# Projection of the per-layer inputs: from the last stage into the prompt's gated linear attention

## The chip, the cores and the metric

The kernel runs on one core of a Trainium2 chip. Its time is the device time of one execution in microseconds (us). A core has a matrix engine (TensorE, here PE, with its weight loads shown apart as PEld), a vector engine (DVE), a scalar engine (ACT), a general engine (POOL), and a sync engine (SP), which here issues most transfers. Each works through its own instructions in order and waits on semaphores for the others.

## What is computed

The program is one step of a decoder layer over a prompt of 1024 tokens and a sample of 8 x 8 tokens: an input projection, gated linear attention (GLA, 4 heads) beside latent attention (8 heads, for the sample over a paged cache of 8192 positions), an output projection, a gated MLP with a short convolution, and at the end the per-layer inputs:

```python
def layer_forward(h, p, pos, gla_s0, conv_prev, attend, lw):
    ...
    o_gla, s_new = gla_chunked(q, k, v, log_a, gla_s0)
    ...
    h = h + jnp.concatenate([o_gla, o_mla], axis=-1) @ lw['w_o']
    y, conv_new = conv_ffn(rmsnorm(h, lw['g_ffn']), conv_prev, lw)
    h = h + y
    h = h + (p.astype(h.dtype) @ lw['ple_w_proj']) * jax.nn.sigmoid(rmsnorm(h, lw['g_ple']) @ lw['ple_w_gate'])
    return h, ckv, krope, s_new, conv_new
```

The product `p @ ple_w_proj` (1024 x 256 by 256 x 1024 for the prompt, 64 x 256 by 256 x 1024 for the sample) depends on nothing else in the layer; its gate depends on nearly everything.

## The kernel before

All matrices are float32. Most products are made of three matmuls of a shorter float32 kind: each operand is split into a high and a low part (`split`, lines 115 to 117: ACT writes the high part, DVE or POOL subtracts), and `mm3` (lines 138 to 141) adds high x high, high x low and low x high in one PSUM bank. Lines 139 to 141 therefore stand for products all over the kernel; one tells them apart by the tile that they write: `ks` (the sample's scores over the cache), `ps_gu` and `ps_dn` (the MLP), `ps_pg` (the last gate), `ps_pj` (the projection, in the last stage).

Two streams are interleaved when the program is written. `dense` is the prompt's work up to the end of its latent attention: the projections in two halves, then GLA, then 8 heads of attention. `cache_stream` is the sample's attention over 64 blocks of the cache; a block has 48 `ks` matmuls with transposes (`ctp`), rope scores (`crp`, `csr`), a softmax (`mt`, `phl`) and a product with the values (`cpv`). Every `yield` of `dense` hands out a weight, and the cache stream takes a step whenever its due time, a step's price times `PACE` of the part, is behind the sum of the weights. The instructions are then ordered on each engine by the scheduler, which moves work of one stream past the other where buffers allow.

GLA runs inside `dense`. `gla_prompt` works on 8 tiles of 128 tokens: `pre` (gates and decays of tile t + 2; loads of gaT, qk and gv), `local` (scores within tile t + 1), `advance` (output `po` and state `pk` of tile t, load of gg), `gla_put` (transposes `pt_go`, store to doT). `gla_sample` is mixed into it a step at a time from the third yield on (`n > GS0`, line 1379). Both take PSUM banks by `pd`, which has three (pool psD); the prompt's attention uses the same three by `pat`.

When `dense` ends, the output projection (`wo_units`, tile `ps_dn`) fills in beside the remaining cache blocks, then come the MLP's two halves (`ff_chunk`, and the seven products of the down projection, tile `ps_dn` again), and then the last stage. Its work on the per-layer inputs stands in three places: `ple_in` loads p (tile `pin`), transposes it (`pt_pl`) and splits it into ph and pl, twice, within the last of the seven products; `ple_proj` loads and splits 256 columns of `ple_w_proj` (wjh, wjl); `ple_unit` does two tiles of 128 tokens and 256 columns at a time: 24 matmuls a tile into `ps_pg`, the sigmoid, 6 matmuls a tile into `ps_pj`, then a multiply and an add on DVE and the store of y_p. `ple_sample` does the same for the sample with 16 + 4 matmuls into one bank. The loop at the end goes over 4 groups of columns, each with 4 pairs of tiles and the sample. All loads and stores there are on SP's queue.

Of the kernel before, what the change touches and what calls it, by code (L numbers as in the profile page):

```python
# [18 lines left out]
P = 128  # L19
D = 1024  # L20
# [25 lines left out]
def step_kernel(ctx: ExitStack, tc: tile.TileContext, A):  # L46
# [46 lines left out]
    doT = dram.tile([D, T], F32, name="doT")  # L93

# [1029 lines left out]

    def gla_prompt(g, wa2, gout, mq, mk):
# [237 lines left out]
    def dense():  # L1363
# [9 lines left out]
        with ExitStack() as s2:  # L1373
            g, g2 = (s2.enter_context(tc.tile_pool(name=nm, bufs=2, reuse_waits="tile")) for nm in ("g", "g2"))
            z["part"] = 4
            sample = gla_sample(g, wa2, *z["gla"])
            for n, w in enumerate(gla_prompt(g2, wa2, *z["gla"])):
                yield w
                if n > GS0:
                    z["part"] = 5  # L1380
                    w2 = next(sample, None)
                    if w2 is not None:
                        yield w2
            for w in sample:
                yield w
# [620 lines left out]
    def ple_in(c):  # L2006

        th, tl = (z["fq"].tile([P, T], F32R, tag="p" + s, name="p" + s, bufs=2) for s in "hl")
        cs = slice(c * P, (c + 1) * P)
        for t0 in (0, 4, 8):  # L2010
            pin = stage([P, 4, P], F32, "pin")
            if t0 < NT:
                n, rows = 4, P
                sp.dma_start(pin, A["p_prompt"][0, 0, t0 * P:(t0 + 4) * P, cs].rearrange("(i p) c -> p i c", p=P))
            else:
                n, rows = 1, R
                sp.dma_start(pin[:R, 0], A["p_sample"][0].rearrange("b t c -> (b t) c")[:, cs])
            pt = p2t([P, 512], "pt_pl")
            w = (n - 1) * P + rows
            for i in range(n):  # L2020
                pe.transpose(pt[:, i * P:i * P + rows], pin[:rows, i], ident[:rows, :rows])
            if t0 < NT:
                split(th[:, t0 * P:t0 * P + w], tl[:, t0 * P:t0 * P + w], pt[:, :w])
            else:
                ts = z["fq"].tile([P, P], F32R, tag="pts", name="pts", bufs=2)
                split(ts[:, :R], ts[:, R:], pt[:, :R])
        return th, tl, ts

# [13 lines left out]
    xn, pT, wpl = {}, [], None  # L2042
    for i, (p, k) in enumerate(steps):
# [28 lines left out]
        elif p == 2:  # L2072
# [6 lines left out]
            if k in (5, 7):  # L2079
                pT.append(ple_in(k // 7))  # L2080
# [21 lines left out]
    def ple_proj(c):  # L2102
        return wload(z["pl"], A["ple_w_proj"][0][:, c * 256:(c + 1) * 256], 2, 256, "wj", 2, st=stg)

    def ple_unit(c, ts, ws):
# [3 lines left out]
        (wj, wg), n = ws, len(ts)  # L2109
# [103 lines left out]
```

## Time and profile before

The profile is of one execution. Its span is what the engines show; the measured time includes a little around it.

| | us |
|---|---|
| runs of the kernel | 2241.42, 2242.73, 2244.2 (median 2242.73) |
| the profiled execution, measured | 2243.74 |
| its span | 2242.0 |
| first output of GLA's prompt tiles (`po`) to the last | 460.6 to 633.6 |
| first and last head's first transpose in the prompt's attention | 651.1, 990.8 |
| first `ps_dn` of the output projection | 1065.1 |
| first `ps_pg`, last `ps_pj` | 2106.7, 2237.8 |

A row of engine time says how long instructions of an engine overlapped the stretch. Matmuls are pipelined, so a row's duration (0.28 us for 256 columns) is longer than the step from one start to the next; what a matmul costs is that step. The PEld share is the time in which weights were being loaded, one load for each matmul.

### The profile page before, as it was taken

The page shows a single profiled execution, that of the slowest core. Times are in us where ns is not written, and L with a number is a line of the kernel's source. Part 1 is how long each engine was busy: PE and PEld are TensorE (multiplying, and loading weights), DVE is VectorE, ACT ScalarE, POOL GpSimd, SP SyncE. Part 2 cuts the span into 40 slices and gives each one's busy share as a digit, 9 for nine tenths or more (in the row PEclk, how much of TensorE's full clock was granted, in tenths as well). Part 3 has the DMA queues.
Part 4 walks back from the last instruction along what each step waited for, and adds up shares of the span by engine and source line. Part 5 has one row for each costly group of instructions (what it writes and reads, how often), then busy time and mean ns, then how long its engine had stood idle before and what let it go on. Part 6 is the DMA issues. An engine that isn't in the chain of part 4 may idle for free.

```text
span 2242.0 us, 38332 instructions
## 1 busy us (share of the span) xinstructions
PE 2140.5 (95%) x13459; PEld 1932.5 (86%) x13459; DVE 1674.3 (75%) x2542; ACT 1360.7 (61%) x3692; POOL 1232.3 (55%) x1320
## 2 busy tenths in 40 slices
PE   7999989999999999999999988999999999998999
PEld 6889978878888888887888877999999998876899
DVE  4775766467788888886878888888888877976632
ACT  5576766777778898887777765434333334434521
POOL 5675667576777777776545558665656560002000
PEclk9899999999999999999999998999999999999999
DMA  5343235413242222212422132323232327667321
GB/s 179 108 144 104 82 115 160 130 56 86 85 126 66 60 60 69 63 56 72 138 78 74 55 117 63 108 90 100 89 100 85 104 72 243 228 173 217 99 77 37
DMA packets 204354, 233.59 MB, mean 104 GB/s; under 512 B 42238, under 2 KB 146147, under 8 KB 204163
## 3 DMA queue, kind: packets, MB, share of 16 engines
q1 hardware_dynamic: 188387, 180.01, 25.6%
q0 software_dynamic: 14544, 46.67, 7.2%
q10 hardware_dynamic: 1232, 4.46, 0.5%
q8 instruction: 108, 1.77, 0.3%
q14 instruction: 83, 0.68, 0.1%
HBM read 188.52 MB, written 42.52 MB: 103 GB/s over the span
## 4 chain that ended last, share of the span: by engine, by line
PE 76%; DVE 8%; ACT 5%; DMA 5%; POOL 3%; issue 2%; SPq 0%; ACTq 0%; DVEq 0%; POOLq 0%
PE ps_gu L140 7%; PE ps_gu L141 7%; PE ps_gu L139 7%; PE ks L139 5%; PE ks L141 4%; PE ks L140 4%; PE cpv L645 2%; PE ctp L522 2%; PE ps_dn L140 2%; PE ps_dn L141 2%; PE ps_dn L139 2%; PE ps_pj L139 2%; PE ps_lt L278 2%; PE ps_pj L140 1%; PE ps_pj L141 1%
## 5 line engine op out<-in xcount | busy, mean ns | idle before, releaser
L560 ACT ACTIVATE csq<-ks 128x256 f32<-128x256 f32 x1040 | 392.5, 400 | 86.7 <-PE ks L141 77.6
L565 DVE TENSOR_REDUCE css<-csq 128x16 f32<-128x1024 f32 (+1 forms) x264 | 315.6, 1196 | 64.6 <-ACT csq L560 63.5
L116 ACT CAST wh<-st 128x512 fp32r<-128x512 f32 x176 | 108.3, 619 | 184.9 <-PE ps_gu L140 164.3
L139 PE MATMUL ks<-mv0h,cTh 128*128 128x320 f32 (+1 forms) x520 | 171.5, 332 | 6.5 <-ACT csq L560 2.9
L139 PE MATMUL ks<-mv1h,cTh 128*128 128x320 f32 (+1 forms) x520 | 169.0, 327 | 7.7 <-ACT sn L562 3.6
L604 POOL TENSOR_TENSOR chl<-craw,chl 128x1024 fp32r<-128x1024 f32 x64 | 141.3, 2207 | 57.2 <-ACT chl L603 56.6
L140 PE MATMUL ks<-mv0l,cTh 128*128 128x320 f32 (+1 forms) x520 | 152.7, 295 | 0.0
L140 PE MATMUL ks<-mv1l,cTh 128*128 128x320 f32 (+1 forms) x520 | 152.6, 295 | 0.0
L141 PE MATMUL ks<-mv0h,cTl 128*128 128x320 f32 (+1 forms) x520 | 148.3, 298 | 0.9 <-DVE cTl L117 0.8
L141 PE MATMUL ks<-mv1h,cTl 128*128 128x320 f32 (+1 forms) x520 | 148.2, 299 | 0.1
L630 POOL TENSOR_TENSOR phl<-sn,phl 128x512 fp32r<-128x512 f32 (+1 forms) x64 | 84.9, 1327 | 106.5 <-ACT phl L629 106.0
L117 DVE TENSOR_TENSOR wl<-st,wh 128x512 fp32r<-128x512 f32 x132 | 119.0, 903 | 28.4 <-ACT wh L116 28.4
L140 PE MATMUL ps_dn<-o 128*128 128x512 f32 x308 | 122.9, 399 | 8.8 <-DVE o L117 8.6
L117 POOL TENSOR_TENSOR wl<-st,wh 128x512 fp32r<-128x512 f32 x44 | 69.5, 1581 | 105.0 <-ACT wh L116 105.0
L141 PE MATMUL ps_dn<-o 128*128 128x512 f32 x308 | 121.2, 394 | 0.0
L117 DVE TENSOR_TENSOR cTl<-ctp,cTh 128x512 fp32r<-128x512 f32 (+1 forms) x136 | 90.0, 662 | 38.9 <-ACT cTh L116 38.0
L562 ACT COPY sn<-ks 128x64 f32<-128x64 f32 x520 | 116.6, 224 | 0.0
L139 PEld LDWEIGHTS ks<-mv0h,cTh 128*128 128x128 f32 x520 | 98.6, 190 | 20.6 <-ACT sn L562 7.3
L139 PEld LDWEIGHTS ks<-mv1h,cTh 128*128 128x128 f32 x520 | 98.5, 189 | 19.7 <-ACT sn L562 7.5
L139 PE MATMUL ps_dn<-o 128*128 128x512 f32 x308 | 109.9, 395 | 5.5 <-ACT o L116 5.5
L1317 POOL TENSOR_TENSOR pl<-p,ph 128x512 fp32r<-128x512 f32 (+1 forms) x96 | 97.4, 1019 | 31.3 <-DVE ph L1316 21.3
L141 PE MATMUL ps_gu<-xrh,wl 128*128 128x320 f32 x352 | 108.7, 309 | 0.0
(674 smaller groups left out, 7881.1 us busy)
## 6 DMA issues: line engine op xcount, KB each, us to landing
raw<-ds SPq DMA_DIRECT2D x77, 256.0 KB
raw<-ffn_w_down SPq DMA_DIRECT2D x66, 256.0 KB
stage<-w_in SPq DMA_DIRECT2D x48, 256.0 KB
st<-ffn_w_gate SPq DMA_DIRECT2D x44, 256.0 KB
st<-ffn_w_up SPq DMA_DIRECT2D x44, 256.0 KB
wr<-ffn_w_down SPq DMA_DIRECT2D x44, 256.0 KB
ds<-cv SPq DMA_DIRECT2D x21, 512.0 KB
oraw<-doT SPq DMA_DIRECT2D x16, 256.0 KB
```

Source lines behind the costliest of these rows:

```text
L116: act.copy(hi, src)
L117: (lo_eng or dve).tensor_tensor(lo, src, hi.bitcast(F32), ALU.subtract)
L139: pe.matmul(ps, ah, bh, start=first, stop=False)
L140: pe.matmul(ps, ah, bl, start=False, stop=False)
L141: return pe.matmul(ps, al, bh, start=False, stop=last)
L278: pe.matmul(ps, x, w, start=first, stop=last)
L560: act.activation(sq[:, f * 256:f * 256 + 256], ks[:, 0:256], AF.Square)
L562: act.copy(o.sn[:, g0 + i, :], ks[:, 256:320])
L565: dve.tensor_reduce(o.ss[:, g0 + i + 1 - n:g0 + i + 1, :].rearrange("p i h -> p (i h)"), sq2[:, :n].rearrange("p i (h n) -> p (i h) n", n= ...
L604: pool.tensor_tensor(ch[:, c0:c1, 128:256], src, ch[:, c0:c1, 0:128].bitcast(F32), ALU.subtract)
L630: pool.tensor_tensor(phl[:, :nt, 64:128], sb, phl[:, :nt, 0:64].bitcast(F32), ALU.subtract)
L1317: pool.tensor_tensor(pl[:, c0:], p[:, c0:], ph[:, c0:].bitcast(F32), ALU.subtract)
```

## The change

The projection of the prompt and the sample is made during GLA by a new generator, `ple_project`, in products of 512 columns; the result goes to two DRAM scratch tensors, `dpj` and `dpjs`. Its weights (2 halves of 512 columns, high and low) take the place of two tiles of `gla_sample` that are done (`qms`, `Ss`), its other tiles rotate with those of `gla_sample` (`gsig`, `gsq`, `go`), and its PSUM banks come from `pd`. In `dense`, once `gla_sample` has nothing left, every yield of `gla_prompt` is followed by two steps of the generator, and what is left runs after it. All its yields have weight 0, so that the cache stream's due times against GLA are as before. In the last stage `ple_in`, `ple_proj` and the `ps_pj` products are gone; `ple_load` reads the product back (tile `pj`, four buffers), two units ahead, and the multiply reads it from there. The loop is written over one list of units, with the same order.

```diff
+    dpj, dpjs = dram.tile([T, D], F32, name="dpj"), dram.tile([R, D], F32, name="dpjs")
...
+    def ple_project(g):
+
+        w = [g.tile([P, 2, 2, 512], F32R, tag=tag, name="wj", bufs=1) for tag in ("qms", "Ss")]
+        for f in range(2):
+            for k in range(2):
+                raw = g.tile([P, 512], F32, tag="gsig", name="wjr")
+                sp.dma_start(raw, A["ple_w_proj"][0][k * P:(k + 1) * P, f * 512:f * 512 + 512])
+                split(w[f][:, 0, k], w[f][:, 1, k], raw, (dve, pool)[k])
+        yield 0.0
+        for t0 in range(0, NT + 1, 2):
+            n, rows = (2, P) if t0 < NT else (1, R)
+            pin = g.tile([P, 2, 256], F32, tag="gsig", name="pin")
+            if t0 < NT:
+                sp.dma_start(pin, A["p_prompt"][0, 0, t0 * P:(t0 + 2) * P, :].rearrange("(i p) c -> p i c", p=P))
+            else:
+                sp.dma_start(pin[:R, 0], A["p_sample"][0].rearrange("b t c -> (b t) c"))
+            for i in range(n):
+                pt = pd([P, 2, P], "pt_pl")
+                for k in range(2):
+                    pe.transpose(pt[:, k, :rows], pin[:rows, i, k * P:(k + 1) * P], ident[:rows, :rows])
+                x = g.tile([P, 2, 2, P], F32R, tag="gsq", name="pT")
...
+                for f in range(2):
+                    ps = pd([P, 512], "ps_pl")
+                    for k in range(2):
+                        if t0 < NT:
+                            mm3(ps, x[:, 0, k], x[:, 1, k], w[f][:, 0, k], w[f][:, 1, k], k == 0, k == 1)
+                        else:
+                            for s_ in range(2):
+                                pe.matmul(ps, x[:, 0, k], w[f][:, s_, k], start=k + s_ == 0, stop=k + s_ == 2)
+                    o = g.tile([P, 512], F32, tag="go", name="pjo")
...
+                        if f:
+                            dve.tensor_copy(o, ps)
+                        else:
+                            act.copy(o, ps)
+                        sp.dma_start(dpj[(t0 + i) * P:(t0 + i + 1) * P, cs], o)
+                    yield 0.0
...
             sample = gla_sample(g, wa2, *z["gla"])
+            early = ple_project(g)
             for n, w in enumerate(gla_prompt(g2, wa2, *z["gla"])):
                 yield w
                 if n > GS0:
...
                     if w2 is not None:
                         yield w2
+                    else:
+                        for _ in range(2):
+                            yield next(early, 0.0)
             for w in sample:
                 yield w
+            for w in early:
+                yield w
...
-            if k in (5, 7):
-                pT.append(ple_in(k // 7))
...
+    def ple_load(c, ts):
+
+        cs, pj = slice(c * 256, c * 256 + 256), pj_room()
+        if ts:
+            t0, n = ts[0], len(ts)
+            sp.dma_start(pj[:, :n], dpj[t0 * P:(t0 + n) * P, cs].rearrange("(i p) c -> p i c", p=P))
+        else:
+            sp.dma_start(pj[:R, 0], dpjs[:, cs])
+        return pj
...
-        for i, t in enumerate(ts):
-            for k in range(2):
-                mm3(pj[:, i], *(x[:, t * P:(t + 1) * P] for x in pT[k][:2]), wj[0][:, k], wj[1][:, k], k == 0, k == 1)
...
+    pjs = [ple_load(c, ts) for c, n, ts in units[:2]]
+    wg = wpl
+    for i, (c, n, ts) in enumerate(units):
+        if i + 2 < len(units):
+            pjs.append(ple_load(units[i + 2][0], units[i + 2][2]))
...
+            ple_unit(c, ts, wg, pjs[i])
```

On PE the first place is GLA, around the state update `pk` of a tile after the sample's work is done. Before:

```order
L1198 MATMUL po<-S,qtb_6135 128x128
L1040 MATMUL pk<-gv,ke 64x128 x4
L1030 MATMUL pt_go<-ident,go 128x128
L139 MATMUL ks<-mv0h,cTh 128x256
L140 MATMUL ks<-mv0l,cTh 128x256
L141 MATMUL ks<-mv0h,cTl 128x256
```

and in the changed kernel, with the projection's `ps_pl` (its lines are numbered one to some fifty higher):

```order
L140 MATMUL ks<-mv0h,cTh 128x320
L141 MATMUL ks<-mv0l,cTh 128x320
L142 MATMUL ks<-mv0h,cTl 128x320
L142 MATMUL ps_pl<-wj,pT 128x512
L140 MATMUL ps_pl<-wj,pT 128x512
L141 MATMUL ps_pl<-wj,pT 128x512
L142 MATMUL ps_pl<-wj,pT 128x512
L1041 MATMUL pk<-gv,ke 64x128 x4
L523 MATMUL ctp<-ident,craw 128x128 x4
```

Four of the projection's matmuls now stand between the tile's output and its state update, together with more `ks` matmuls than before.

The second place, on PE too, is the last head of the prompt's attention, from the second half of its first operand's transposes (`t<-ident,ldq`) on. Before:

```order
L1262 MATMUL t<-ident,ldq 96x128 x4
L522 MATMUL ctp<-ident,craw 128x128 x3
L139 MATMUL ks<-mv1h,cTh 128x256
L140 MATMUL ks<-mv1l,cTh 128x256
L141 MATMUL ks<-mv1h,cTl 128x256
L139 MATMUL ks<-mv1h,cTh 128x320
L140 MATMUL ks<-mv1l,cTh 128x320
L141 MATMUL ks<-mv1h,cTl 128x320
```

and now:

```order
L1310 MATMUL t<-ident,ldq 96x128 x4
L1370 MATMUL o<-ph,vo_9702 128x512
L1371 MATMUL o<-ph,vo_9702 64x512
L1370 MATMUL o<-ph,vo_9702 128x512
L1371 MATMUL o<-ph,vo_9702 64x512
L1310 MATMUL t<-ident,ldk 96x128 x4
L140 MATMUL csr<-qbd0h,kTh 128x64
L141 MATMUL csr<-qbd0l,kTh 128x64
L142 MATMUL csr<-qbd0h,kTl 128x64
```

The `ks` matmuls that went along with the last head before have been placed earlier, in GLA; the last head now stands with hardly any.

More of the change, by code (lines that the diff above doesn't have):

```diff
@@ L2004, in ple_gate @@
                       "gu", 2, st=stg) for i in range(2)]
[L2006 to L2027, printed above, removed]
     z["xs"].tile([P, 2, 512], F32, tag="r", name="raw2", bufs=5)
@@ new lines, in step_kernel @@
+    pjs = [ple_load(c, ts) for c, n, ts in units[:2]]
[3 more added lines that the diff above has]
+            pjs.append(ple_load(units[i + 2][0], units[i + 2][2]))
+        if n == 0 and c:
+            wg = nxt
+        if ts:
+            ple_unit(c, ts, wg, pjs[i])
+        else:
+            ple_sample(c, wg, pjs[i])
+        if c == 0 and n < 2:
+            for t in (2 * n, 2 * n + 1):
+                turned(t, xn[t])
+                if not n:
+                    xn[t + 2] = normalised(t + 2)
+        if c == 1 and n == 1:
+            conv_out()
+        if n == 1 and c < 3:
+            nxt = ple_gate(c + 1)
```

61 lines of the change are left out of this document (26 added, 35 removed).

## The prediction

> **What bounds the kernel now.** The page comes first, for the span and for how much of it each engine is busy.
>
> ```profile
> span 2242.0 us, 38332 instructions
> PE 2140.5 (95%) x13459; PEld 1932.5 (86%) x13459; DVE 1674.3 (75%) x2542; ACT 1360.7 (61%) x3692; POOL 1232.3 (55%) x1320
> ```
>
> TensorE (PE) is busy for 95% of the span, but the ends of its matmuls are modelled; the weight loads (PEld) at 86% leave room. How much, and where, is read from the busy time by stretches: the last six tiles of the prompt's gated linear attention (545 to 651 us), five heads of the latent attention beside the cache stream (736 to 991), the end of that attention (1024.4 to 1052.6), and the last stage (2106 to 2238).
>
> ```profile
> core 0: us, PE busy (x) PEld busy (x) DVE busy (x) ACT busy (x) POOL busy (x), PEclk, DMA share, GB/s
> 545.00:651.00 106.00, 104.35 (x779) 90.62 (x779) 83.65 (x142) 81.18 (x266) 73.47 (x95) 1.00 0.36 97
> 736.00:991.00 255.00, 250.06 (x1721) 218.37 (x1720) 212.88 (x351) 222.76 (x665) 188.15 (x192) 1.00 0.23 65
> 1024.40:1052.60 28.20, 24.23 (x128) 19.34 (x126) 16.06 (x27) 16.76 (x35) 23.08 (x23) 0.88 0.14 38
> 2106.00:2238.00 132.00, 132.00 (x1101) 131.51 (x1099) 50.60 (x80) 36.98 (x71) 5.47 (x7) 1.00 0.21 67
> ```
>
> In the last stage the weight loads fill 131.51 of 132 us: every matmul taken out there shortens the kernel by its own pitch, since vector, scalar engine and DMA are under 40%. In the linear attention PEld is at 90.62/106 = 85.5%, in the five heads at 218.37/255 = 85.6%, so some 15 us of PE time are open in the 106 us that receive the new work. At 1024.4 to 1052.6, where PE runs out of cache work, it is at 69% and the granted clock falls to 0.88. Next, the chain of waits of the last stage:
>
> ```profile
> by line: PE ps_pg L141 22.4%; PE ps_pg L140 22.3%; PE ps_pg L139 22.3%; PE ps_pg L2137 7.7%; PE ps_pj L141 6.2%; PE ps_pj L140 6.1%; PE ps_pj L139 6.1%; PE pt L132 3.5%; PE pt_co L2094 0.4%; DVE sg L2122 0.3%; DVE sg L2123 0.3%; issue 0.1%;
> ```
>
> It is nearly all PE, and 18.4% of it is the projection that the change takes away.
>
> **What is removed from the last stage.** The tiles' view gives the counts, the timeline the pitch (start to start, not the duration).
>
> ```profile
> L139 PE MATMUL ps_pj<-wjh,ph x64: 280/283/283, 2118.9 to 2237.5; 128*128 128x256 f32 x64
> L140 PE MATMUL ps_pj<-wjl,ph x64: 283/283/283, 2119.7 to 2237.6; 128*128 128x256 f32 x64
> L141 PE MATMUL ps_pj<-wjh,pl x64: 279/283/283, 2119.9 to 2237.8; 128*128 128x256 f32 x64
> L2137 PE MATMUL ps_pg<-wjh,pts x8: 283/283/283, 2122.9 to 2223.2; 128*128 128x256 f32 x8
> L2137 PE MATMUL ps_pg<-wjl,pts x8: 283/283/286, 2123.0 to 2223.4; 128*128 128x256 f32 x8
> L2021 PE MATMUL pt_pl<-ident,pin x18: 270/272/273, 2097.2 to 2113.6; 128*128 128x128 f32 x16, 64*128 64x64 f32 x2
> ```
> ```profile
> 2150.22 0.28 PE L139 MATMUL ps_pg<-guh,xg 128*128 128x256 f32 x1
> 2150.34 0.28 PE L140 MATMUL ps_pg<-gul,xg 128*128 128x256 f32 x1
> ...
> 2097.18 1.03 PE L2021 MATMUL pt_pl<-ident,pin 128*128 128x128 f32 x8
> 2097.97 0.48 PE L141 MATMUL ps_dn<-o 128*128 128x512 f32 x1
> ...
> 2098.52 0.39 PE L140 MATMUL ps_dn<-o 128*128 128x512 f32 x1
> 2098.75 0.39 PE L141 MATMUL ps_dn<-o 128*128 128x512 f32 x1
> 2098.97 0.39 PE L139 MATMUL ps_dn<-o 128*128 128x512 f32 x1
> 2099.20 0.39 PE L140 MATMUL ps_dn<-o 128*128 128x512 f32 x1
> ```
>
> A 256-wide matmul takes 0.120 us, a 512-wide one 0.227 (0.68 over three), a transpose 0.79/8 = 0.099. Removed: 3 x 64 + 16 = 208 matmuls, 208 x 0.120 = 25.0 us, and 18 x 0.099 = 1.8 us. The very last product also goes:
>
> ```profile
> 2237.35 0.38 ACT L2117 ACTIVATE sg<-ps_pg 128x256 f32<-128x256 f32 x1 [3.22 <-PE ps_pg L141]
> ...
> 2237.75 0.28 PE L141 MATMUL ps_pj<-wjh,pl 128*128 128x256 f32 x1
> 2238.13 0.42 DVE L2122 TENSOR_TENSOR sg<-sg,ps_pj 128x256 f32<-128x256 f32 x1 [2.72 <-PE ps_pj L141]
> ...
> 2239.03 0.34 SPq L2124 DMA_DIRECT2D y_p<-sg  x1
> ```
>
> The multiply waits for it till 2238.13, while the sigmoid ended at 2237.73: 0.4 us more. **Last stage: -27.2 us.** The splits of the pin and wj tiles (ACT, DVE) and their loads lie under PE; their removal counts as nothing. The 21 added pj loads (about 4 MB) cost nothing either: DMA is at 0.21, each is issued ahead of its use by a unit or more on SP, and only DVE waits for one, not PE, since the sigmoid alone empties the PSUM bank. Without that cover the last one would cost some 3 us, as the last store does from its issue at 2239.03 to the span's end.
>
> **What is added to the linear attention.** On PE 96 + 8 matmuls of 512 columns, 104 x 0.227 = 23.6 us, and the same 18 transposes, 1.8: 25.4 us. So PE saves 1.8 us by the wider form; all else depends on whether the 25.4 find open time. Lower bound: they fill the open time of the six tiles wholly (106 - 90.6 = 15.4) and cost 10.0. Upper bound of the ordinary kind: the share stays at 85.5% and they cost 25.4/0.855 = 29.7. Five heads, which have plenty of independent cache work beside them, do not get above 85.6% either; more cover has not raised the share here. I take 28, near that end. ACT gets some 12 us (four weight splits, nine turned tiles, ten evictions, at 0.4 to 0.6 us each), DVE some 10, POOL two splits. The prices come from these:
>
> ```profile
> L560 ACT ACTIVATE csq<-ks 128x256 f32<-128x256 f32 x1040 | 392.5, 400 | 86.7 <-PE ks L141 77.6
> L116 ACT CAST ph<-pt_pl x4: 586/587/592, 2097.8 to 2113.5; 128x512 fp32r<-128x512 f32 x4
> L117 DVE TENSOR_TENSOR pl<-pt_pl,ph x4: 679/686/692, 2098.4 to 2114.2; 128x512 fp32r<-128x512 f32 x4
> L117 POOL TENSOR_TENSOR wl<-st,wh 128x512 fp32r<-128x512 f32 x44 | 69.5, 1581 | 105.0 <-ACT wh L116 105.0
> ```
>
> (81.18 + 12)/134 and (83.65 + 10)/134 stay at 70%, so neither becomes the bound. Moved past SP's queue are four weight loads, five of p and eighteen stores; the stores stand between the loads of gaT, qk and gv, and each waits for its eviction. A late eviction holds back the next tile's inputs; at DMA share 0.36 and two tiles of lead I price this at nothing, and at its worst in the rivals.
>
> **What that does to the cache stream.** In the order of the change, 1449 ks matmuls stand ahead of the first transpose of the latent attention, 1293 before: 156 (3.25 cache blocks) have slipped forward, because the linear attention yields to the new work and the cache fills in. Where the next stage begins both have 2376, so the lead is given back at the end: attention then runs with no ks matmul for 261 matmuls in a row, where it was 123. The slipped blocks cost the same in both places (85.5% and 85.6%). The bare stretch does not:
>
> ```profile
> 1025.67 0.39 PE L1278 MATMUL t<-kh,qh 96*128 96x256 f32 x1 [0.79 <-DVE amx L1281]
> ...
> 1028.06 0.44 PE L1278 MATMUL t<-kh,qh 96*128 96x384 f32 x1 [0.82 <-DVE amx L1281]
> ...
> 1029.72 2.09 PE L645 MATMUL cpv<-chl,phl 128*128 128x258 f32 x8 [1.15 <-POOL phl L630]
> ```
>
> With no cache matmuls between, PE waits for DVE's maxima and POOL's splits. 123 matmuls took 28.2 us, 0.229 each; the 138 more would take 31.6 there, against 31.6 x 0.686/0.856 = 25.3 under cover: +6.3 us. From below it is nothing, if POOL, which still had cache work in this stretch, is what held it; from above 12, if the clock stays low for all of it. I take 6.
>
> [...]
>
> **Sum:** -27.2 + 28 + 6 = +7 us (6.8). The profiled run's span is 2242.0 and its time 2243.74, 1.7 outside the span; the runs' median is 2242.73. On the median: 2249.5 us.
>
> **Rivals.** (1) *The open time takes it up.* The sample's linear attention has ended before the new work starts, and the new matmuls depend on nothing in the recurrence; if PE is held there by the recurrence's waits, they fall into them: -27.2 + 10 + 4 = -13, 2229.5 us. It decides once the new work costs less than 21 of its 25.4 us. For it: 15.4 open us. Against it: 85.6% with plenty of cover, and that PE executes in order. [...] (2) *Even:* new work about 20, bare stretch 6: within 0.2% (4.5 us, about what a measurement of this kernel can tell from no change), 2242. (3) *The recurrence is held up.* The new work takes PSUM banks from the same three (psD), and its stores stand ahead of gaT on SP; if PEld falls to 78%, (90.6 + 25.4)/0.78 - 106 = +43, in all +21, 2264. For it: nine bank uses of a tile become some fourteen. Against it: the order already spaces the steps. (4) *The last stage doesn't get shorter,* because gate weights or pj come late: -15 instead of -27, 2262. Against it: DVE 38%, DMA 0.21.
>
> **Chances.** Forecast (slower by 4.5 to 15 us) 0.40; rival 1 0.26; rival 2 0.17; rival 3 0.13; rival 4 0.04. Faster 0.26, same 0.17, slower 0.57. The range, 2226 to 2266, reaches just past rival 1 and rival 3 and leaves about a tenth out at each end; the forecast's own is 2247 to 2258.
>
> **What would show it.** A last stage that holds no product but ps_pg, at a PEld share near 100%, and is shorter by 27 us from the last ps_dn to the end: first term. The time from the start of the linear attention's third tile to the first ps_dn, grown by 32 to 36 us: the others. PEld above 90% between the first ps_pl and the last po means rival 1; below 80%, with gaT or qk loads ending PE's waits, rival 3. The bare stretch should take 55 to 62 us with a clock under 0.95. The forecast is wrong if that whole middle grows by less than 23 us.

## Result: 28 us slower, and where it went

| runs | median us | lowest to highest |
|---|---|---|
| before, beside the change | 2242.53 | 2241.42 to 2244.2 |
| the change | 2270.72 | 2268.36 to 2273.5 |

The ratio is 1.0126, with a 95% interval of 1.0108 to 1.0143. The profiled execution of the change took 2269.04 us, its span is 2267.3. The page's first lines show no engine that became the bound: PE and its weight loads have, within a point, the shares that they had.

```profile
span 2267.3 us, 38244 instructions
PE 2151.4 (95%) x13355; PEld 1931.7 (85%) x13355; DVE 1673.4 (74%) x2553; ACT 1364.9 (60%) x3705; POOL 1234.7 (54%) x1322
```

The loss has to be found by stages. The next two fences are the busy time by stretches, cut at the same events in both kernels: from the third tile's first `po` (the expectations of e6 and e10 call it the fourth) to the first head's first transpose; from there to the first `ps_dn` of the output projection; from there to the first `ps_gu`. In both fences the third row is the bare stretch at the end of the latent attention, in which no `ks` matmul starts; the fence after the change ends with the last stage. After the change:

```profile
core 0: us, PE busy (x) PEld busy (x) DVE busy (x) ACT busy (x) POOL busy (x), PEclk, DMA share, GB/s
545.00:717.90 172.90, 165.15 (x1158) 144.05 (x1157) 126.19 (x215) 126.76 (x403) 106.00 (x127) 0.99 0.35 104
717.90:1112.70 394.80, 375.49 (x2473) 320.15 (x2472) 299.28 (x503) 319.81 (x929) 277.73 (x285) 0.97 0.23 67
1040.40:1100.60 60.20, 53.96 (x266) 38.90 (x265) 29.13 (x56) 32.34 (x67) 39.79 (x42) 0.86 0.09 23
1112.70:1421.20 308.50, 277.56 (x1672) 240.58 (x1670) 254.01 (x381) 223.26 (x671) 160.97 (x139) 0.96 0.26 85
2159.20:2264.00 104.80, 104.13 (x870) 103.84 (x868) 44.84 (x72) 29.92 (x60) 6.08 (x7) 1.00 0.32 101
```

And the same stages before, where the prediction showed others:

```profile
542.30:651.10 108.80, 107.15 (x801) 93.23 (x800) 85.29 (x147) 82.78 (x271) 76.27 (x99) 1.00 0.36 96
651.10:1065.10 414.00, 399.87 (x2718) 349.07 (x2716) 338.01 (x549) 353.75 (x1044) 305.59 (x311) 0.99 0.24 69
1024.40:1052.50 28.10, 24.12 (x126) 19.24 (x125) 15.96 (x27) 16.76 (x35) 22.98 (x23) 0.88 0.14 38
1065.10:1365.90 300.80, 276.89 (x1671) 241.09 (x1669) 252.54 (x381) 223.12 (x671) 162.00 (x139) 0.96 0.27 87
```

| stretch | before | change | difference | the prediction's price |
|---|---|---|---|---|
| to the third tile's first `po` | 542.3 | 545.0 | +2.7 | 0 |
| linear attention | 108.8 | 172.9 | +64.1 | +34 for the linear and the latent together |
| latent attention | 414.0 | 394.8 | -19.2 | (in the row above) |
| output projection | 300.8 | 308.5 | +7.7 | 0 |
| first `ps_gu` to the last `ps_dn` | 740.5 | 738.0 | -2.5 | 0 |
| last `ps_dn` to the end | 135.6 | 108.1 | -27.5 | -27.2 |

The differences add up to +25.3, the difference of the spans; by the medians the change costs 28.2, and where the other 2.9 lie one profile of each kernel doesn't show. Two things carry the miss of 18.5 us in the spans: the two attentions together grew by 44.9 instead of 34, and the output projection by 7.7 instead of nothing.

The cache stream's share of each stretch is read from the same view with the tile `ks` alone; 48 `ks` matmuls are one block, and a row may count one to three that only overlap its edge. After the change:

```profile
545.00:717.90 172.90, 78.73 (x450) 63.09 (x450) 58.44 (x220) 0.99 0.35 104
717.90:1112.70 394.80, 164.72 (x929) 136.61 (x927) 125.55 (x466) 0.97 0.23 67
1112.70:1421.20 308.50, 128.37 (x746) 106.48 (x744) 100.79 (x375) 0.96 0.26 85
```

Before:

```profile
542.30:651.10 108.80, 54.52 (x297) 41.80 (x297) 40.13 (x148) 1.00 0.36 96
651.10:1065.10 414.00, 194.88 (x1083) 160.02 (x1083) 145.97 (x541) 0.99 0.24 69
1065.10:1365.90 300.80, 128.13 (x746) 106.91 (x744) 101.05 (x375) 0.96 0.27 87
```

The slip is there as foretold: 153 `ks` more in the linear attention, 156 fewer in the latent one, the same number beside the output projection. The last stage is as foretold too; its chain of waits holds no product but `ps_pg`:

```profile
by line: PE ps_pg L142 29.2%; PE ps_pg L140 29.2%; PE ps_pg L141 29.2%; PE ps_pg L2169 7.3%; PE pt L133 3.3%; PE pt_co L2123 0.4%; DVE sg L2158 0.4%; ACT sg L2156 0.4%; PE ps_dn L141 0.2%; PE ps_dn L142 0.2%; PE ps_dn L140 0.2%; issue 0.0%
```

### The profile page after: what moved, and what is told of

Read it like the earlier page. It is cut to its first block, busy times and chain, and to the rows that moved or that the text cites. A ratio compares the mean times of both kernels' runs of the same rounds, so it can differ in the third digit from the quotient of the medians.

```text
span 2267.3 us, 38244 instructions
## 1 busy us (share of the span) xinstructions
PE 2151.4 (95%) x13355; PEld 1931.7 (85%) x13355; DVE 1673.4 (74%) x2553; ACT 1364.9 (60%) x3705; POOL 1234.7 (54%) x1322
## 4 chain that ended last, share of the span: by engine, by line
PE 74%; DVE 10%; ACT 6%; DMA 5%; issue 2%; POOL 2%; SPq 0%; DVEq 0%; POOLq 0%; ACTq 0%
PE ps_gu L141 7%; PE ps_gu L142 7%; PE ps_gu L140 7%; PE ks L140 5%; PE ks L142 4%; PE ks L141 4%; PE cpv L646 2%; PE ctp L523 2%; PE ps_dn L141 2%; PE ps_dn L142 2%; DVE css L566 2%; PE ps_dn L140 2%; PE ps_lt L279 2%; PE ps_pg L142 1%; PE ps_pg L141 1%
## 5 line engine op out<-in xcount | busy, mean ns | idle before, releaser
L140 PE MATMUL ks<-mv1h,cTh 128*128 128x320 f32 (+1 forms) x520 | 167.4, 324 | 10.2 <-ACT sn L563 3.7
L140 PEld LDWEIGHTS ks<-mv0h,cTh 128*128 128x128 f32 x520 | 98.5, 189 | 24.7 <-ACT sn L563 9.5
L140 PEld LDWEIGHTS ks<-mv1h,cTh 128*128 128x128 f32 x520 | 98.5, 189 | 21.2 <-ACT sn L563 7.6
L593 POOL TENSOR_TENSOR sn<-sn,cy 128x512 f32<-128x512 f32 (+1 forms) x64 | 70.6, 1103 | 72.1 <-DVE cy L591 61.4
```

What stands on the lines that cost most here:

```text
L140: pe.matmul(ps, ah, bh, start=first, stop=False)
L593: pool.tensor_tensor(snv, snv, y[:, :nt].rearrange("p i h -> p (i h)").unsqueeze(2).broadcast_to([P, nt * 8, 8]), ALU.mult)
```

## The experiments

Two theories stood at the start. A: the loss is PE work at full price, and cache blocks that slip with it. B: it lies in what surrounds the new matmuls, the PSUM banks that they share with the recurrence and their stores on SP's queue. In the table, "linear", "latent" and "output" are the three stretches above, with the number of `ks` matmuls that start in each. The stretches are read from one profiled execution of each kernel; that of e5, e6, e10 and e14 took 3.5 to 5.4 us more than the kernel's median, so a difference of a few us between stretches of these is not safe.

| kernel | median us | linear | latent | output | longest run without `ks`, us |
|---|---|---|---|---|---|
| before | 2242.5 | 108.8 (297) | 414.0 (1083) | 300.8 (744) | 28.2 |
| the change | 2270.7 | 172.9 (450) | 394.8 (927) | 308.5 (744) | 60.2 |
| e1 tail only | 2213.4 | 108.7 (297) | 413.9 (1083) | 300.9 (744) | 27.8 |
| e2 linear attention only | 2302.4 | 172.8 (450) | 394.7 (927) | 311.1 (744) | 60.2 |
| e3 pace 0.90 | 2258.8 | 172.7 (450) | 412.6 (1053) | 278.5 (618) | 27.0 |
| e4 in the latent attention | 2269.4 | 108.8 (297) | 468.5 (1083) | 303.9 (744) | 54.0 |
| e5 one of three | 2252.9 | 142.3 (369) | 405.6 (1008) | 312.9 (744) | 29.9 |
| e6 no stores | 2271.8 | 175.4 (450) | 394.9 (927) | 310.3 (744) | 60.1 |
| e7 other banks | 2282.6 | 195.0 (462) | 388.3 (915) | 302.7 (744) | 67.9 |
| e8 before, pace 0.90 | 2253.1 | 108.7 (297) | 445.9 (1209) | 280.0 (618) | 6.0 |
| e9 before, pace 1.2 | 2263.5 | 108.7 (297) | 398.6 (987) | 334.0 (840) | 47.6 |
| e10 before, held back | 2261.0 | 98.5 (267) | 408.5 (1023) | 335.1 (840) | 29.6 |
| e11 change, paced | 2242.9 | 145.6 (354) | 413.3 (1053) | 291.9 (714) | 29.9 |
| e12 as e11, all steps at once | 2246.1 | 145.5 (345) | 413.4 (1062) | 292.5 (714) | 22.1 |
| e13 as e11, one of three | 2234.0 | 135.5 (354) | 409.4 (1053) | 293.9 (714) | 29.6 |
| e14 before, paced | 2242.4 | 107.2 (300) | 428.9 (1140) | 292.9 (690) | 12.2 |

The kernel before ran beside each group of experiments, with medians of 2244.5 (e1 to e4), 2246.0 (e5 to e8), 2245.6 (e9 to e11), 2245.3 (e12) and 2244.9 (e13, e14).

### The two halves of the change, each alone

e1 keeps the changed last stage and leaves the projection out; the last stage reads the raw p in place of the product. e2 makes the projection there and keeps the last stage of before.

```diff
-            early = ple_project(g)
...
-            for w in early:
-                yield w
...
-            sp.dma_start(pj[:, :n], dpj[t0 * P:(t0 + n) * P, cs].rearrange("(i p) c -> p i c", p=P))
+            sp.dma_start(pj[:, :n], A["p_prompt"][0, 0, t0 * P:(t0 + n) * P, :].rearrange("(i p) c -> p i c", p=P))
```

> The changed last stage alone; the linear attention is as before. The projection is left out: pj is read from p itself, with transfers of the same size. Theory A (the inserted work pays its full PE price because PE is full beside it, and it spends the cache cover early, so that the end of the attention runs bare): the middle is as before, first ps_dn at 1065, first ps_gu at 1366, and only the last stage is shorter, by 30 us as in the changed kernel: 2212 to 2214 us. Theory B (the inserted work holds up the linear attention's recurrence through PSUM banks and SP's queue): the same here. Theory C (the last stage gains less than its matmuls because pj or the gate's weights come late): 2220 or more. If the stretch from the first ps_dn to the first ps_gu is 301 us here, its 7.7 us in the changed kernel belong to the insertion or to chance.

Measured: 2213.36 us, ratio 0.9864 (0.9843 to 0.9885); its span of 2209.3 is 32.7 under that of before.

```diff
+            early = ple_project(g)
...
+                    else:
+                        for _ in range(2):
+                            yield next(early, 0.0)
```

> The projection made in the linear attention and stored, while the last stage makes it once more as before. Theories A and B: the middle as in the changed kernel, first ps_gu some 55 us later than before, 2296 to 2300 us; e1 and e2 add up to the change (-30 and +55). If the output projection's stretch is 301 us here and not 308, the total is 2290 and those 7.7 us are chance.

Measured: 2302.37 us, ratio 1.026 (1.0235 to 1.0284), 2.4 us above the range; a span of 2300.4, 58.4 over that of before. The two add up to +25.7, the change to +25.3: nothing of the loss lies between the halves. The new last stage brings some 30 us; to make the projection in the linear attention costs some 58. A view by stretches of e1's last stage shows that the loads of the product cost nothing there, at 102.25 us of weight loads in 104.40:

```profile
2102.60:2207.00 104.40, 102.46 (x858) 102.25 (x856) 43.79 (x70) 29.67 (x59) 5.22 (x5) 1.00 0.33 102
```

### The stretch without cache work, covered again

e3 is the change with the cache stream's price factor in the latent attention lowered, so that more blocks come there.

```diff
-PACE = [1.41, 1.088, 1.601, 1.168, 1.142, 0.708, 1.035, 1.027]
+PACE = [1.41, 1.088, 1.601, 1.168, 1.142, 0.708, 0.90, 1.027]
```

> The change with PACE of the attention at 0.90 instead of 1.035, so that more cache steps are handed out beside the attention: by the order the run of matmuls without ks at its end falls from 261 to 123, as before, and 126 fewer ks are left for the output projection. Theory A: the linear attention stays at 172 us; the bare stretch falls from 60 to about 28 us; against the change 6 to 14 us faster, 2257 to 2265, unless the output projection now runs bare. Theory B: the bare stretch costs little by itself, 2267 to 2273.

Measured: 2258.79 us, ratio 1.0068 (1.0045 to 1.009). The stretch fell from 60.2 to 27.0 us, the latent attention grew by 17.8 with 126 more `ks`, the output projection shrank by 30.0 with as many fewer. That is 12 us back of 28 (14, if each kernel is compared with the kernel before that ran beside it). Whether the factor helps any kernel was asked by the same edit on the kernel before:

> The kernel before with the cache stream's price factor in the prompt's latent attention at 0.90 in place of 1.035, as in the run of the change with that factor (2258.8 us, 12 under the change; its bare stretch fell from 60 to 27 us). In its order 2502 ks matmuls stand ahead of the output projection (2376 before) and the longest run without ks is 30 matmuls (123 before). If that gain came from covering the 138 matmuls that the change had laid bare, the kernel before, with little bare, gains at most 3 us or loses: 2240 to 2250 us. If the factor helps whatever the kernel, it gains the same 10 to 13: 2230 to 2233.

Measured: 2253.13 us, ratio 1.0028 (1.0017 to 1.0039): 7 us slower, beyond the range that either reading gave. The factor alone is a loss, and in the change it is a gain. For the same 126 `ks` the latent attention paid 17.8 us in e3 and 31.9 here, which goes with the bare stretch that they cover in e3; but the output projection gave back 30.0 in e3 and only 20.8 here, and the bare stretch does not explain that.

### The projection as cover for the bare stretch

e4 puts the projection into the end of the latent attention, a step a yield from yield 280 of 304 on, with tiles of that attention's pool. The linear attention is that of before.

```diff
-            early = ple_project(g)
...
-            yield from prompt_attention(ap)
+            early = ple_project(ap)
+            for n, w in enumerate(prompt_attention(ap)):
+                yield w
+                if n >= 280:
+                    for _ in range(1):
+                        yield next(early, 0.0)
+            for w in early:
+                yield w
```

> The projection moved from the linear attention to the last heads of the prompt's attention, from the 280th of its 304 yields on, one step for each; the linear attention is as before, the last stage as in the change. Theory A: it lies in the stretch of 28 us where before PEld was at 69% and the clock at 0.88, fills some 9 us of open time and costs 14 to 20 us; the last stage gives 30: 2226 to 2233 us, faster than both. Theory B: attention takes its PSUM banks from the same three, so it is held up as the recurrence was: the middle grows by 35 us or more, 2247 or more.

Measured: 2269.43 us, ratio 1.011 (1.0089 to 1.0131), far above the 2226 to 2233 that A had given. The busy time by stretches, for the bare one and for the wait behind it:

```profile
1041.90:1095.80 53.90, 48.80 (x232) 37.05 (x230) 21.65 (x38) 24.14 (x50) 23.27 (x26) 0.94 0.33 109
1095.80:1119.00 23.20, 16.57 (x86) 14.36 (x86) 13.79 (x21) 14.47 (x47) 5.37 (x10) 0.78 0.80 283
```

The stretch had 28.2 us before and has 53.9 with 25.4 us of new PE work in it: the two did not overlap at all, though weight loads had been at 69% there. A share of 69% was not 31% of open time: a 512-wide matmul of the projection loads its weights for 0.188 us (the median of the weight loads of `ps_pl` in e4) and takes 0.227 from start to start, so a stretch full of such matmuls would show an estimated 83%. POOL was the busiest engine beside PE in this stretch (23.08 of 28.2 us before); PE work laid beside it saved nothing (53.9 us, for 28.2 and 25.4). From the end of the bare stretch to the first `ps_dn`, 12.6 us became 21.3 (1095.8 to 1117.1; the row above runs to 1119). The timelines of PE and ACT show what waited: PE twice for the next cache block, the second time while ACT, which writes that block's `sn`, sat waiting for a load of the output projection.

```profile
1104.03 0.41 PE L140 MATMUL ks<-mv0h,cTh 128*128 128x320 f32 x1 [3.01 <-ACT cTh L117]
...
1109.39 0.58 PE L140 MATMUL ks<-mv0h,cTh 128*128 128x256 f32 x1 [3.09 <-ACT sn L563]
```
```profile
1108.33 0.62 ACT L117 CAST sh<-oraw 128x512 fp32r<-128x512 f32 x1 [3.91 <-DMA oraw<-doT]
```

The first head also took 41.2 us instead of 31.2, with a wait of 4.7 on DVE's `amx`, and the last head's part ahead of the bare stretch 45.7 instead of 33.6, with more cache work in it (129 `ks` instead of 94); why the first head began worse was not followed up.

### What surrounds the new matmuls

Three edits of the change: one matmul instead of three in each product of the prompt, no stores, other PSUM banks.

```diff
-                            mm3(ps, x[:, 0, k], x[:, 1, k], w[f][:, 0, k], w[f][:, 1, k], k == 0, k == 1)
+                            pe.matmul(ps, x[:, 0, k], w[f][:, 0, k], start=k == 0, stop=k == 1)
```

> The changed kernel with one matmul instead of three in each prompt product of the projection (high x high only; the two products with a low part are left out). 64 of 104 ps_pl matmuls go, 64 x 0.227 = 14.5 us of PE; tiles, splits, PSUM banks, evictions, loads and stores stay. In its order 1368 ks matmuls stand ahead of the latent attention (1449 in the change, 1293 before), and the longest run without ks is 135 matmuls (261, 123). Theory A (the new work pays its full PE price, and the cache blocks that slip with it cost more than they give back): less work and half the slip; against the change -17 for the work (14.5/0.855), -13 for the bare stretch and its slip, in all 2238 to 2246 us. Theory B (banks, evictions and the SP queue hold up the recurrence, not the PE time): 2262 to 2271.

Measured: 2252.9 us, ratio 1.0026 (1.0015 to 1.0038), between the two ranges. 14.5 of the 25.4 us of PE work, and with it half of the slip, bought back 18 of 28 us (21 by the kernels beside each), less than A and more than B had. The latent attention, with 1.56 blocks fewer than before and no longer bare stretch, gave back 8.4 us.

```diff
-                        sp.dma_start(dpj[(t0 + i) * P:(t0 + i + 1) * P, cs], o)
...
-                        sp.dma_start(dpjs[:, cs], o[:R])
```

> The changed kernel without the 18 stores of the product (the product isn't kept; the last stage multiplies by the raw inputs p, read over the same number of loads). The order on PE is that of the change: 1449 ks ahead of the latent attention, 261 matmuls in the bare stretch. Theory A (PE price and slip): no change, 2267 to 2274 us. Theory B (stores on SP's queue ahead of gaT, qk and gv hold up the recurrence): the linear attention from its fourth tile to the first head falls from 173 us towards 150, in all 2245 to 2255.

Here the last stage reads the raw p, as in e1. Measured: 2271.81 us, ratio 1.0099 (1.0067 to 1.013), the linear attention at 175.4 where B had it fall towards 150. No cost of the stores on SP's queue shows; that half of B falls.

```diff
-                pt = pd([P, 2, P], "pt_pl")
+                pt = pm([P, 2, P], "pt_pl")
...
-                    ps = pd([P, 512], "ps_pl")
+                    ps = pm([P, 512], "ps_pl")
```

> The changed kernel with the projection's PSUM banks taken from the cache stream's pool (psM) in place of the linear attention's three (psD). In its order 1461 ks matmuls stand ahead of the latent attention and the longest run without ks is 290 matmuls. Theory B (the third rival of the prediction: the new work takes the recurrence's banks): the linear attention shortens by 10 us or more, in all 2250 to 2262 us. Theory A (PE price and slip): the banks are no limit; the linear attention within 3 us of 173, the bare stretch 5 to 7 us longer for 29 more matmuls, of which half is paid: 2269 to 2278.

Measured: 2282.55 us, ratio 1.0161 (1.0139 to 1.0182), slower than both ranges. The tiles' view of the recurrence's output, first with these banks, then in the change:

```profile
L1246 PE MATMUL po<-S,qtb x56: 270/275/275, 519.5 to 649.2; 128*128 128x128 f32 x56
```
```profile
L1246 PE MATMUL po<-S,qtb x56: 270/275/275, 518.2 to 703.5; 128*128 128x128 f32 x56
```

With these banks the recurrence's last output comes 54 us earlier; but the projection's `ps_pl` then ran from 626.5 to 733.2 instead of 576.3 to 705.1, so the recurrence also had fewer matmuls between its steps, and how much of the 54 us the shared banks had cost is not separated. The first head began at 741.3 instead of 717.9, since projection and cache blocks then followed the recurrence instead of lying in it. The recurrence's end is not what sets the time of this stretch.

### What a cache block costs, and where

By now the blocks were suspect: after e1 to e7, each one that left the latent attention had returned 5.4 to 7.3 us (8.4/1.56 in e5, 19.2/3.25 in the change, 25.7/3.5 in e7). Theory M takes that for a property of the attention, theory S holds to the price in the prediction. e9 and e10 move blocks by the price factors of the kernel before, with no projection near.

```diff
-PACE = [1.41, 1.088, 1.601, 1.168, 1.142, 0.708, 1.035, 1.027]
+PACE = [1.41, 1.088, 1.601, 1.168, 1.142, 0.708, 1.2, 1.027]
```

> The kernel before with the cache stream's price factor in the prompt's latent attention at 1.2 in place of 1.035: two cache blocks (96 ks matmuls) fewer beside that attention, two more beside the output projection; the linear attention as before. The longest run without ks is 218 matmuls (123 before). It asks what a cache block gives back when it leaves the attention, with no projection near. Theory M (the attention has waits of its own that a block partly fills: a block returns some 6 us, as 1.56 and 3.25 fewer blocks did): the stretch from the first head to the first ps_dn falls from 414.0 to 401 to 404 us. Theory S (a block returns its full share, 9.5/0.855 = 11.1 us, less 4.4 us for 95 more matmuls laid bare, which is the price in the prediction): 394 to 397. In both the output projection takes the two blocks at 8 to 11 us each; in all 2246 to 2257 us by M, 2240 to 2247 by S.

Measured: 2263.52 us, ratio 1.0088 (1.0064 to 1.0112). The row of `ks` in the latent attention:

```profile
653.10:1051.70 398.60, 176.25 (x987) 145.36 (x987) 132.27 (x494) 0.99 0.24 69
```

The stretch fell to 398.6, between the two theories: 7.7 us a block. The whole is slower than both had it, since the output projection took the two blocks at 16.6 each, not at 8 to 11.

```diff
-PACE = [1.41, 1.088, 1.601, 1.168, 1.142, 0.708, 1.035, 1.027]
+PACE = [1.41, 1.088, 1.601, 1.168, 1.5, 1.1, 0.90, 1.027]
```

> The kernel before with the cache stream's price factors at 1.5 and 1.1 (for 1.142 and 0.708) in the linear attention and 0.90 (for 1.035) in the latent one: 36 ks matmuls (0.75 block) fewer beside the linear attention, 1.25 blocks fewer beside the latent one, two more beside the output projection. It asks for the price of a block in the linear attention, with no projection near. If it is the full 11.1 us there, the stretch from the fourth tile's first po to the first head falls from 108.8 to 100 to 101 us; if the recurrence's own waits are partly filled by it, to 103 to 106. The latent attention falls by 7 to 8 us by theory M (6 us a block), by 11 to 13 by theory S. In all 2243 to 2253 us.

Measured: 2261.0 us, ratio 1.0072 (1.0052 to 1.0092). The view by stretches of `ks` in this kernel:

```profile
545.80:644.30 98.50, 47.73 (x269) 37.49 (x267) 35.81 (x132) 1.00 0.37 103
644.30:1052.80 408.50, 182.36 (x1024) 150.71 (x1023) 138.06 (x514) 0.98 0.24 67
1052.80:1387.90 335.10, 144.37 (x842) 120.07 (x840) 114.55 (x423) 0.95 0.26 82
```

In the linear attention 30 `ks` fewer, 0.62 block, save 10.3 us, more than the full price; in the latent one 1.25 blocks return only 5.5 us, under both theories; the output projection pays 34.3 for two, which also puts the whole above its range. So a block's price differs by a factor of two to four with what it lies beside, in a kernel that knows no projection.

### The slip undone

e11 is the change with factors that hold the cache stream back in the linear attention and let it on in the latent one.

```diff
-PACE = [1.41, 1.088, 1.601, 1.168, 1.142, 0.708, 1.035, 1.027]
+PACE = [1.41, 1.088, 1.601, 1.168, 1.6, 1.1, 0.8, 1.027]
```

> The changed kernel with the cache stream held back in the linear attention and let on in the latent one (factors 1.6, 1.1 and 0.80 for 1.142, 0.708 and 1.035): 1353 ks matmuls ahead of the latent attention (1449 in the change, 1293 before), 2406 ahead of the output projection (2376 in both), longest run without ks 129 matmuls (261, 123). It undoes most of the slip and keeps the projection. Theory M: the stretch to the first head falls by 2 x 11 from 173 to 149 to 153 us, the latent attention grows by 16 from 394.9 to 409 to 413, the output projection falls by 5 to 7: 2255 to 2261 us, still above the kernel before. If the slip were all of the loss: 2240 to 2250.

Measured: 2242.88 us, ratio 0.9995 (0.9983 to 1.0007): even with the kernel before, 28 us under the change. That is the range of "the slip is all of the loss".

```profile
542.70:688.30 145.60, 62.69 (x356) 49.59 (x354) 47.52 (x178) 1.00 0.39 117
688.30:1101.60 413.30, 190.82 (x1053) 156.98 (x1053) 140.75 (x527) 0.98 0.25 71
1101.60:1393.50 291.90, 121.87 (x716) 103.19 (x714) 96.99 (x360) 0.96 0.26 84
```

Against the change, the linear attention has 96 `ks` fewer, two blocks, and is 27.3 us shorter (13.7 each); the latent one has 126 more and is 18.5 longer (7.0 each); the output projection has 30 fewer and is 16.6 shorter. Order alone, at the same work, is worth 28 us here. Not all of it is the slip between the two attentions: together they are 8.8 us shorter, with 0.62 block taken over from the output projection, and the other 16.6 are in the output projection, which has these 0.62 block fewer than in either kernel.

e12 takes the projection's steps all at once, to bring the last blocks out of the linear attention:

```diff
-                        for _ in range(2):
+                        for _ in range(40):
```

> The kernel of the run before (the change with the factors 1.6, 1.1 and 0.80; 2242.88 us) with all steps of the projection taken at once when the sample's linear attention has ended, in place of two after each yield. 1344 ks matmuls stand ahead of the latent attention (1353), 2406 ahead of the output projection (the same), the longest run without ks is 98 matmuls (129). With the prices of a cache block as the runs so far give them (13.6 us in the linear attention with the projection, 5 to 7 in the latent one): 0.19 block less in the first, -2.6 us, as much more in the second, +1.2; nothing else moves: 2239 to 2244 us, even with the kernel before or 0.3% under it. If taking the steps at once holds the recurrence up (its last output later than 672.7 us), 2245 to 2260.

Measured: 2246.1 us, ratio 1.0009 (0.9996 to 1.0021), linear attention 145.5: no gain over e11, 2 us above its range, and no version that beats the kernel before.

Two questions were left. What do the new matmuls cost when no block moves? e13 has e11's order with one matmul of three:

> The change with the factors 1.6, 1.1 and 0.80 (2242.88 us) and one matmul instead of three in each prompt product of the projection (high x high only; the two products with a low part are left out). Its cache order is that of the run with three: 1353 and 2406 ks matmuls, 129 without ks. 64 x 0.227 = 14.5 us of PE work go at a fixed cache share. If the new matmuls pay the full price of the prediction (14.5/0.855 = 17), the stretch to the first head falls from 145.6 to 128 to 130 us and the whole to 2224 to 2229. If they partly fall into open time there (20.6 us for 25.4, as the line through the change and the paced run has it, 0.81 each), it falls by 11 to 13, to 133 to 135, and the whole to 2229 to 2234. If the cache stream and the recurrence set the time and the matmuls are nearly free, by under 6: 2237 to 2245.

Measured: 2234.04 us, ratio 0.9948 (0.9934 to 0.9963). The number of `ks` in each stretch is that of e11:

```profile
544.10:679.60 135.50, 63.97 (x356) 50.04 (x354) 47.71 (x179) 1.00 0.42 126
```

14.5 us of PE work taken out shorten the linear attention by 10.1 us, a little less than the middle reading, 0.70 us for each us; the whole by 8.8. And do such factors help any kernel? e14 gives the kernel before 1.6, 1.0 and 0.8 (e11 had 1.1 for the second):

> The kernel before with the factors 1.6, 1.0 and 0.80 (for 1.142, 0.708 and 1.035), near those that brought the change from 2270.7 to 2242.9 us: 1290 ks matmuls ahead of the latent attention (1293 before), 2430 ahead of the output projection (2376), longest run without ks 63 matmuls (123). If the paced change gained by undoing the slip: the kernel before has no slip to undo; 1.2 blocks more in the latent attention at 12 us are +14, as many fewer in the output projection at 8 to 14 are -10 to -16: 2241 to 2252 us. If the factors help any kernel: 2215 to 2225.

Measured: 2242.43 us, ratio 0.9988 (0.9975 to 1.0): 2.4 us under its neighbours. So e11's 28 us are no gain that these factors bring to any kernel; they come with the order that the change had disturbed. The latent attention pays 14.9 us there for 1.19 blocks more, 12.5 each, as e8 did (31.9 for 2.63, 12.1 each): blocks beyond the share of before cost some twice what blocks under it return.

## Why the prediction missed, step by step

**The last stage** was right: -27.5 us from the last `ps_dn` to the end, for -27.2, without a wait on the loads of the product. That the two agree within 0.3 us is in part luck: half of the transposes that the sum counts (1.8 us for all 18) stood ahead of the last `ps_dn`.

**The bare stretch** was right in its time: 60.2 us at a clock of 0.86, for 55 to 62 under 0.95. Its price was not quite. It grew by 32.1 us with 19.7 us more of weight loads (38.90 and 19.24), which at 85.5% would take 23.0: +9.1, where the prediction took 6.

**That the slipped blocks "cost the same in both places (85.5% and 85.6%)" is the step that failed.** The PEld share of a stretch is an average; what a block costs when it comes, or returns when it goes, is another number. The rows above let the step be priced by the weight loads alone. In the linear attention these grew by 50.8 us, 59.4 at 85.5%, and the stretch grew by 64.1: 4.7 more. In the latent attention outside its bare stretch they fell by 48.6 us (329.83 of 385.9 us, 85.5%, became 281.25 of 334.6, 84.1%), 56.8 at 85.5%, and only 51.3 came back: 5.5 less. These 10.2 us (of the 4.7, a part may be the new work's) are what the prediction put at nothing, and nearly the miss in the two attentions (44.9 for 34, 10.9); the rest is the bare stretch's 3.1 too little against 2.4 too much for the new work, whose 21.9 us of weight loads (50.8 - 28.9) make 25.6 at 85.5%, for the 28 taken.

That a block returns less from the latent attention than its share, with no projection near, e9 shows (7.7 us a block, where its full share is 11.1, or 8.9 with the price that the prediction puts on the longer bare stretch) and e10 (4.4, with a bare stretch as long as before). That it costs more than its share in the linear attention is what e10 (10.3 us for 0.62 block) and e11 (13.7 us a block) say. Why it does, and why the latent attention gives so little back, was not settled.

**The new work's 28 us** was too much as well, if e13 holds for the change: at its 0.70 the 25.4 us cost an estimated 17.8. Then the slipped blocks carry more of the linear attention's 64.1 us: 3.2 of them at the 13.7 of e11 are 44, and with the 19.2 that came back the two attentions would have grown by 42, for 44.9 measured. So the open time may have taken some of the new work up, as the first rival had it, but that rival took the rest of the bill for 4 us. How the 64.1 us divide between new work and blocks in the change itself no run shows; e13 has e11's order.

**The output projection** was counted at nothing, since its blocks are the same. It grew by 7.7 us. With 744 `ks` there, it took 300.8 to 312.9 us over eight kernels (before, the change, e1, e2, e4 to e7), and this is not chance alone: PE runs the same 1669 matmuls in the same order there, by their tiles, in the kernel before and e1 (300.8 and 300.9 us), and in another order, again the same, in the change, e2 and e6 (308.5, 311.1 and 310.3). In the change, 4.8 of the 7.7 us have come up when the last `ps_dn` starts (277.2 us after the first, for 272.5), 2.9 come behind it. Which of the displaced instructions costs the time is open.

**The third rival,** that the recurrence is held up, is seen in part (in e7, with other banks and another order, the recurrence ends 54 us earlier), but its price is not: e7 is slower than the change, and the stores show no cost (e6). PEld from the first `ps_pl` to the last `po` of the change is neither above 90% nor below 80%:

```profile
576.20:703.50 127.30, 123.85 (x854) 107.97 (x853) 87.07 (x152) 92.17 (x294) 73.49 (x88) 0.99 0.32 99
```

107.97 of 127.30 is 84.8%, so the signs that the prediction gave for its rivals said nothing, while the total was off by 18.5: the share of a stretch was too coarse a gauge.

## What to carry to other kernels

Price moved work by what a stretch loses or gains when that work alone is put in or taken out, not by the stretch's mean share; two runs with other price factors, before the change was made, would have shown that a block's price depends on the place (e9 and e10: 4.4 to 17 us). Work that is put into one of two interleaved streams at weight nothing also moves the other stream: count what slips, and ask what it was covering where it came from. A change of this kind should be judged after the order is tuned again, since order alone was worth as much (28 us) as the whole gain in the last stage; even so, tuned (e11), the change was only even with the kernel before.

## What was unexpected of the hardware

In the change's bare stretch the granted clock falls to 0.50 in pieces of some 5 to 10 us, in which PE is busy for 94 to 100%. The view by stretches, in steps of 5 us, and the timeline of PE:

```profile
1040.00:1045.00 5.00, 3.00 (x17) 2.16 (x16) 1.98 (x3) 2.73 (x8) 4.51 (x10) 0.90 0.00 0
1045.00:1050.00 5.00, 4.75 (x18) 3.82 (x18) 3.97 (x6) 1.93 (x4) 5.00 (x5) 0.50 0.12 26
1075.00:1080.00 5.00, 4.60 (x27) 3.33 (x25) 3.17 (x7) 2.82 (x5) 3.05 (x4) 1.00 0.00 0
1080.00:1085.00 5.00, 3.64 (x21) 2.25 (x20) 2.87 (x6) 1.64 (x4) 0.73 (x1) 1.00 0.12 26
1085.00:1090.00 5.00, 4.71 (x12) 3.22 (x13) 0.86 (x3) 2.68 (x5) 1.46 (x2) 0.50 0.00 0
1090.00:1095.00 5.00, 5.00 (x14) 3.46 (x13) 0.88 (x2) 2.05 (x4) 2.78 (x3) 0.50 0.13 30
```
```profile
1042.03 0.39 PE L1373 MATMUL o<-pl,vo 128*128 128x256 f32 x1 [1.40 <-POOL pl L1365]
...
1091.32 0.63 PE L1370 MATMUL o<-ph,vo 128*128 128x512 f32 x1
1091.74 0.63 PE L1371 MATMUL o<-ph,vo 128*64 128x512 f32 x1
...
1096.69 0.39 PE L1370 MATMUL o<-ph,vo 128*128 128x512 f32 x1
1096.92 0.40 PE L1371 MATMUL o<-ph,vo 128*64 128x512 f32 x1
```

At 1091 a 512-wide matmul takes 0.42 us from start to start, at 1096 it takes 0.23. No gap on PE in the stretch is longer than 1.40 us (1.67 from one start to the next); both falls come behind a piece in which PE was busy for only 60 or 73%. The mean of 0.86 over 60.2 us amounts to 8.4 us at the full clock; how much of that the kernel would get back is not shown, since PE also waits for other engines there (1.40 us for POOL's `pl` ahead of 1042.03). What makes the clock fall was not shown: no run here tests it.

The spread of one kernel's runs goes with the clock as well: of e12's twelve runs, the shortest had a span of 2239.2 us at a mean clock of 0.986, the longest 2254.2 at 0.979. Differences of less than some 5 us in this kernel need several runs on each side.
